# A depthwise convolution's shifted copies: through memory on GpSimd's queue, with two pointwise blocks ahead of the first convolution block

## The chip, the cores and the metric

The kernel runs on one core of a Trainium2 chip. The metric is the device time of one execution in microseconds (us); times of several runs are given as their median with the lowest and the highest. Engines are named as the profile names them: PE (TensorE), PEld (its weight loads), DVE (VectorE), ACT (ScalarE), POOL (GpSimd), SP (SyncE, which here only issues DMAs).

## The reference, cut to what matters

The reference is a decoder trunk of two layers on 256 positions of width 1024, in fp32. Each layer is a gated feed-forward network (FFN), a mixer, and another FFN, each with an adaLN modulation. The mixer of the second layer is a Conformer convolution module, and the change lies there:

```python
def conformer_conv(h, w_pw1, b_pw1, w_dw, b_dw, ln_g, ln_b, w_pw2, b_pw2):
    u = h @ w_pw1 + b_pw1                       # 1024 -> 2048
    a, g = jnp.split(u, 2, axis=-1)
    u = a * jax.nn.sigmoid(g)                   # GLU
    u = conv_general_dilated(u, w_dw[:, None, :], padding=[(30, 0)],
                             feature_group_count=1024) + b_dw   # depthwise, causal, width 31
    u = jax.nn.silu(layer_norm(u, ln_g, ln_b))
    return u @ w_pw2 + b_pw2
```

## The kernel before

The program's order on each engine is the order in which the Python code emits it (a manual schedule). All weights come from memory in one stream of half units of 512 KB. `issue` (line 191) asks for the next piece on SP's queue into one of six `raw` tiles (`RAW`), and `step` (line 208) consumes one: a weight is split into a rounded part `whi` (ACT, line 245) and a remainder `wlo` (DVE, line 220), an adaLN piece is folded into a sum by DVE (lines 284 and 286). Each `step` issues the piece six places on, whose slot it has just emptied. `high_part` emits the ACT copy up to one piece ahead of the step. The split units live in a ring of six (`RING`), and a unit can enter only when the unit six places before it has been used up (`uses`). `block` takes as many steps as a quota that `take` sets, and is called in each block of matmuls.

In `conv` the 1024 channels are eight blocks of 128. For a block b:

- `U(b)` (b from 4) or `UT` (b below 4) computes both halves of the first pointwise product `pw1` into PSUM. `U` takes one of two banks named `u`.
- `glu(b)` makes the sigmoid on ACT (`sg`, line 1065) and the gated product on DVE into one of four `ub` tiles (line 1066): 288 columns, 30 of them zeros ahead of the 256 positions.
- `spread(b)` makes the layout that the convolution wants: `R[b]`, in which the partitions are four shifts j of 32 channels, and the free axis is four groups g of channels. It is 16 DMAs from SBUF to SBUF, each 32 partitions by 284 columns, half on SP's queue and half on POOL's (line 1077).
- `wide(b)` expands the block's taps on POOL into `wd[b]` (line 1019; three buffers).
- `C(b)` is the convolution: 64 small matmuls over R[b] and wd[b] (line 1085), for a whole block or a half (128 positions), and an eviction with the bias on ACT into `v` (line 1089).
- `VT(b)` transposes `v` back (line 1099) for the layer norm's statistics.

SP's queue thus holds the weight stream and half of the spreads, in the order of the program. The blocks 0 to 3 pass `glu`, `spread` and `wide` ahead of the loop; the loop over b from 0 to 3 runs U(b + 4), glu(b + 4), C(b), spread(b + 4), wide(b + 3) and VT(b - 1); C(4) to C(7) follow, the last three in halves.

Of the kernel before, what the change touches and what calls it, by code (L numbers as in the profile page):

```python
# [8 lines left out]
F32 = mybir.dt.float32  # L9
# [5 lines left out]
P = 128  # L15
# [19 lines left out]
class Unit:  # L35
# [5 lines left out]
    def __init__(self, parts, uses=2):  # L41
        self.parts, self.uses = parts, uses
        self.hi = self.lo = None
        self.ready = 0
# [12 lines left out]
class Trunk:  # L57
    def __init__(self, ctx, tc, a):
        self.tc, self.nc, self.a = tc, tc.nc, a

        def pool(name, bufs=1, **kw):
            return ctx.enter_context(tc.tile_pool(name=name, bufs=bufs, **kw))

        self.const = pool("const")
        self.tiny = pool("tiny", 2)
        pool("pad").tile([P, 256], F32, name="pad")
        self.rawp = pool("rawp", RAW)
        self.hlp = pool("hlp", RING)
        self.keep = pool("keep")
        self.two = pool("two", 2)  # L70
        self.ps = pool("ps", 1, space=bass.MemoryType.PSUM)
        self.vecs = {(l, s, k): Vec(l, s, k) for l in range(2) for s in range(3) for k in range(3)}
        self.sums, self.open, self.pend, self.naccs = [], [], [], 0
        self.phase = 0
        self.ss, self.rs, self.zs = {}, {}, {}
        self.quota = self.credit = 0
        self.plan()
# [189 lines left out]
    def take(self, n=None):  # L267
        self.quota = PUMP[self.phase] if n is None else n
# [731 lines left out]
    def conv(self, cp, before, after):  # L1000
        nc, a = self.nc, self.a
        b1, bdw = self.col["b1"], self.col["bdw"]
        lng, lnb = self.col["lng"], self.col["lnb"]
        cols, take = self.cols, self.take
# [5 lines left out]
        ub = [cp.tile([P, 288], F32, name=f"ub{i}") for i in range(4)]  # L1010
# [4 lines left out]
        us, R, wd, yv, st, mv, rs = {}, {}, {}, {}, {}, {}, {}  # L1015

        def wide(b):
            wd[b] = cp.tile([P, 8, 4, 32], F32, name="wd", tag="wd", bufs=3)
            nc.gpsimd.tensor_tensor(
                wd[b], self.w2[:, :, 4 * b : 4 * b + 4].unsqueeze(3).to_broadcast([P, 8, 4, 32]),  # L1020
                mask.unsqueeze(1).unsqueeze(1).to_broadcast([P, 8, 4, 32]), op=ALU.mult,
            )

        def U(b):
            unit = self.pw1[b]
            self.need(unit)
            self.block()
            us[b] = self.bank("u")
            for s in range(2):
                out = us[b][:, s * T : s * T + T]  # L1030
                for k in range(KT):
                    cs = slice(k * 256 + s * P, k * 256 + s * P + P)
                    self.mm3(out, unit.hi[:, cs], unit.lo[:, cs], self.hh[:, k, :], self.hl[:, k, :], k == 0, k == KT - 1)
            unit.uses -= 1

        def UT(ps, b, t):

            unit = self.pw1[b]
            self.need(unit)
            self.block()  # L1040
            ts = slice(t * P, t * P + P)
            for k in range(KT):
                cs = slice(k * 256, k * 256 + 256)
                self.mm3(ps, self.hh[:, k, ts], self.hl[:, k, ts], unit.hi[:, cs], unit.lo[:, cs], k == 0, k == KT - 1)
            unit.uses -= 1

        def evac(ps):
            e = self.two.tile([P, 512], F32, name="z", tag="z", bufs=3)
            nc.scalar.activation(e, ps, AF.Copy)
            return e  # L1050

        def across(b, t, e, c):

            if b not in us:
                us[b] = self.bank("u")
            for s in range(2):
                nc.tensor.transpose(
                    us[b][:, s * T + t * P : s * T + t * P + P], e[:, c + s * P : c + s * P + P], self.ident
                )

        def glu(b):
            ps = us.pop(b)
            u = ub[b % 4]
            sg = cp.tile([P, T], F32, name="sg", tag="sg", bufs=2)
            nc.scalar.activation(sg, ps[:, T:], AF.Sigmoid, bias=cols[:, b1 + 8 + b : b1 + 9 + b])
            nc.vector.scalar_tensor_tensor(
                u[:, 30:286], ps[:, 0:T], cols[:, b1 + b : b1 + b + 1], sg, op0=ALU.add, op1=ALU.mult
            )

        def spread(b):  # L1070

            u = ub[b % 4]
            R[b] = cp.tile([P, 4, 284], F32, name="R", tag="R", bufs=4)
            for g in range(4):
                for j in range(4):
                    eng = nc.sync if (g + j) % 2 else nc.gpsimd
                    eng.dma_start(R[b][32 * j : 32 * j + 32, g, :], u[32 * g : 32 * g + 32, j : j + 284])  # L1077

        def C(b, t0=0, n=T):
            if ("v", b) not in us:  # L1080
                us["v", b] = cp.tile([P, T], F32, name="v", tag="v", bufs=3)
            ps = self.bank("m")[:, 0:n]
            for q in range(8):
                for g in range(4):
                    nc.tensor.matmul(  # L1085
                        ps[32 * g : 32 * g + 32, :], wd[b][:, q, g, :], R[b][:, g, 4 * q + t0 : 4 * q + t0 + n],
                        start=q == 0, stop=q == 7,
                    )
            nc.scalar.activation(
                us["v", b][:, t0 : t0 + n], ps, AF.Identity, bias=cols[:, bdw + b : bdw + b + 1]  # L1090
            )

        def VT(b, ts=(0, 1)):
            v = us["v", b]
            h, i = b // 4, b % 4
            for t in ts:
                if i == 0:
                    yv[t, h] = self.bank("y")
                nc.tensor.transpose(yv[t, h][:, i * P : i * P + P], v[:, t * P : t * P + P], self.ident)
            if i == 3:  # L1100
                for t in ts:
                    if h == 0:
                        st[t] = cp.tile([P, 2, 6], F32, name=f"st{t}")
                    nc.vector.bn_stats(st[t][:, h, :], yv[t, h])

        def moments(t):
            mv[t] = cp.tile([P, 2], F32, name=f"mv{t}")
            rs[t] = cp.tile([P, 1], F32, name=f"lr{t}")
            nc.vector.bn_aggr(mv[t], st[t])
            nc.vector.tensor_scalar(rs[t], mv[t][:, 1:2], EPS, None, op0=ALU.add)  # L1110
            nc.gpsimd.tensor_tensor(rs[t], rs[t], self.mhalf[:, 0:1], op=ALU.pow)

        def norm(t, h):
            z = self.two.tile([P, 512], F32, name="z", tag="z", bufs=3)
            nc.vector.tensor_scalar(z, yv[t, h], mv[t][:, 0:1], rs[t], op0=ALU.subtract, op1=ALU.mult)
            self.zs[t, h] = z
# [49 lines left out]
        UT(w[1][:, 256:], 2, 1)  # L1166
        across(0, 1, e, 0), across(1, 1, e, 256)
        e = evac(w[1])
        glu(0), spread(0), wide(0)
        UT(w[3][:, 256:], 3, 1)  # L1170
        f = evac(w[3])
        across(2, 0, e, 0), across(2, 1, e, 256)
        glu(1), spread(1), wide(1)
        across(3, 0, f, 0), across(3, 1, f, 256)
        glu(2), spread(2), wide(2)
        glu(3), spread(3)
        take(PUMP_LOOP)
        for b in range(4):
            U(b + 4)
            glu(b + 4)  # L1180
            C(b)
            spread(b + 4), wide(b + 3)
            if b:
                VT(b - 1)
                if b == 1:
                    nc.vector.tensor_tensor(b2, b2, gate, op=ALU.mult)
                else:
                    x = self.x[b - 2]
                    nc.vector.tensor_tensor(x, x, b2, op=ALU.add)
        nc.scalar.activation(warm, self.mhalf, AF.Silu)  # L1190
        self.block()
        C(4), wide(7), VT(3)
        self.need(self.pw2[3])
        take(5)
        C(5, 0, P), VT(4), self.block(), C(6, 0, P), VT(5, (0,)), C(7, 0, P), VT(6, (0,))
        C(5, P, P), VT(7, (0,)), moments(0), norm(0, 0), norm(0, 1)
        take(0)
        C(6, P, P), VT(5, (1,)), C(7, P, P), VT(6, (1,)), swish(0, 0), VT(7, (1,)), moments(1), put(0, 0)
# [64 lines left out]
```

## Time and profile before

| | |
|---|---|
| three runs, median (lowest to highest) | 1057.43 us (1055.07 to 1059.31) |
| the profiled execution, its own time | 1057.27 us |
| its span in the profile | 1055.5 us |
| PE, DVE, ACT, POOL busy, share of the span | 97%, 74%, 46%, 8% |
| moved by DMA | 254.92 MB, mean 242 GB/s |

The span is what the profile covers from the first instruction to the last; the execution's own time is 1.8 us longer. A busy share is a mean over the whole kernel. The convolution, at about 735 to 860 us, is one stage of it, and its own limits are read from that stretch of the trace.

### The profile page before, as it was taken

The page shows a single profiled execution, that of the slowest core. Times are in us where ns is not written, and L with a number is a line of the kernel's source. Part 1 is how long each engine was busy: PE and PEld are TensorE (multiplying, and loading weights), DVE is VectorE, ACT ScalarE, POOL GpSimd, SP SyncE. Part 2 cuts the span into 40 slices and gives each one's busy share as a digit, 9 for nine tenths or more (in the row PEclk, how much of TensorE's full clock was granted, in tenths as well). Part 3 has the DMA queues.
Part 4 walks back from the last instruction along what each step waited for, and adds up shares of the span by engine and source line. Part 5 has one row for each costly group of instructions (what it writes and reads, how often), then busy time and mean ns, then how long its engine had stood idle before and what let it go on. Part 6 is the DMA issues. An engine that isn't in the chain of part 4 may idle for free.

```text
span 1055.5 us, 14925 instructions
## 1 busy us (share of the span) xinstructions
PE 1020.3 (97%) x5510; PEld 826.7 (78%) x5510; DVE 785.3 (74%) x1165; ACT 489.6 (46%) x763; POOL 86.8 (8%) x149
## 2 busy tenths in 40 slices
PE   8999999999999999999999999999995899999998
PEld 5778787877776788878878878888984688888886
DVE  5679888978997798878578878776747669556643
ACT  3454444555685544444454444454621356434420
POOL 3000000002210000000020000000484200000000
PEclk9999999999999999999999999999998999999999
DMA  8989999948676399999739889894667427776711
GB/s 299 316 273 333 305 341 321 324 140 284 220 241 194 106 329 313 308 309 315 233 105 315 290 297 312 276 307 136 193 201 227 159 80 259 259 234 193 231 40 40
DMA packets 186812, 254.92 MB, mean 242 GB/s; under 512 B 10437, under 2 KB 136166, under 8 KB 186740
## 3 DMA queue, kind: packets, MB, share of 16 engines
q1 hardware_dynamic: 183856, 250.88, 72.1%
q0 software_dynamic: 2736, 3.04, 1.0%
q8 instruction: 43, 0.70, 0.3%
q14 instruction: 29, 0.24, 0.1%
q10 hardware_dynamic: 148, 0.06, 0.0%
HBM read 248.24 MB, written 1.05 MB: 236 GB/s over the span
## 4 chain that ended last, share of the span: by engine, by line
PE 79%; DVE 7%; DMA 5%; ACT 3%; issue 3%; POOL 2%; SPq 1%; DVEq 0%; ACTq 0%; POOLq 0%
PE u L666 14%; PE u L664 14%; PE u L665 14%; PE y L664 10%; PE y L666 10%; PE y L665 10%; DMA raw<-in_ffn_w_in_dram 2%; DMA raw<-in_ada_w_dram 2%; DVE wlo L220 2%; PE m L742 2%; ACT whi L245 1%; POOL R L1077 1%; PE m L1085 1%; ACT p L893 1%; DVE x L601 1%
## 5 line engine op out<-in xcount | busy, mean ns | idle before, releaser
L220 DVE TENSOR_TENSOR wlo<-raw,whi 128x1024 fp32r<-128x1024 f32 x320 | 389.2, 1244 | 51.1 <-ACT whi L245 50.8
L245 ACT ACTIVATE whi<-raw 128x1024 fp32r<-128x1024 f32 x320 | 329.1, 1055 | 178.1 <-DMA raw<-in_ffn_w_in_dram 96.2
L664 PE MATMUL u<-whi,hh 128*128 128x512 f32 x672 | 266.7, 397 | 1.2 <-ACT hh L587 1.2
L666 PE MATMUL u<-whi,hl 128*128 128x512 f32 x672 | 263.1, 391 | 0.0
L665 PE MATMUL u<-wlo,hh 128*128 128x512 f32 x672 | 261.8, 390 | 0.0
L286 DVE SCALAR_TENSOR_TENSOR acc<-raw,sc,acc 128x512 f32<-128x512 f32 x224 | 168.0, 750 | 6.7 <-DMA raw<-in_ada_w_dram 1.7
L666 PEld LDWEIGHTS u<-whi,hl 128*128 128x128 f32 x672 | 126.1, 188 | 29.6 <-DVE hl L588 1.7
L664 PEld LDWEIGHTS u<-whi,hh 128*128 128x128 f32 x672 | 126.2, 188 | 28.7 <-ACT hh L587 2.9
L665 PEld LDWEIGHTS u<-wlo,hh 128*128 128x128 f32 x672 | 126.4, 188 | 25.0
L664 PE MATMUL y<-whi,gh 128*128 128x512 f32 x352 | 138.5, 393 | 0.2 <-ACT gh L750 0.2
L666 PE MATMUL y<-whi,gl 128*128 128x512 f32 x352 | 137.3, 390 | 0.0
L665 PE MATMUL y<-wlo,gh 128*128 128x512 f32 x352 | 137.1, 389 | 0.0
L664 PE MATMUL y<-whi,hh 128*128 128x512 f32 (+1 forms) x256 | 96.9, 379 | 0.2 <-ACT hh L934 0.2
L666 PE MATMUL y<-whi,hl 128*128 128x512 f32 (+1 forms) x256 | 93.9, 367 | 0.0
L665 PE MATMUL y<-wlo,hh 128*128 128x512 f32 (+1 forms) x256 | 93.5, 365 | 0.0
L751 DVE TENSOR_TENSOR gl<-m,gh 128x512 fp32r<-128x512 f32 (+1 forms) x48 | 31.0, 647 | 83.7 <-ACT gh L750 83.5
L750 ACT ACTIVATE gh<-m 128x512 fp32r<-128x512 f32 (+1 forms) x48 | 27.0, 563 | 131.9 <-PE m L742 131.8
L712 ACT ACTIVATE sg<-u 128x256 f32<-128x256 f32 x84 | 32.1, 383 | 106.6 <-PE u L666 106.6
L664 PEld LDWEIGHTS y<-whi,gh 128*128 128x128 f32 x352 | 66.1, 188 | 15.7 <-ACT sg L712 1.7
L666 PEld LDWEIGHTS y<-whi,gl 128*128 128x128 f32 x352 | 66.1, 188 | 14.4 <-DVE gl L751 0.4
L665 PEld LDWEIGHTS y<-wlo,gh 128*128 128x128 f32 x352 | 66.1, 188 | 13.4
L620 POOL TENSOR_TENSOR r<-v,mhalf 128x1 f32<-128x1 f32 x12 | 6.6, 554 | 671.9 <-DVE v L619 671.9
(169 smaller groups left out, 944.6 us busy)
## 6 DMA issues: line engine op xcount, KB each, us to landing
raw<-in_ffn_w_in_dram SPq DMA_DIRECT2D x164, 512.0 KB, 5.1
raw<-in_ada_w_dram SPq DMA_DIRECT2D x144, 512.0 KB, 5.1
raw<-in_ffn_w_out_dram SPq DMA_DIRECT2D x88, 512.0 KB, 5.3
raw<-in_attn_w_qkv_dram SPq DMA_DIRECT2D x24, 512.0 KB, 4.9
raw<-in_conv_w_pw_dram SPq DMA_DIRECT2D x24, 512.0 KB, 5.1
raw<-in_ffn_w_in_dram SPq DMA_DIRECT2D x24, 256.0 KB, 5.7
raw<-in_attn_w_o_dram SPq DMA_DIRECT2D x8, 512.0 KB, 4.3
gate<-in_ada_b_dram SPq DMA_DIRECT2D x6, 512.0 KB, 6.7
```

The costliest lines, as they stand in the source:

```text
L220: (eng or nc.vector).tensor_tensor(lo, raw, hi.bitcast(F32), op=ALU.subtract)
L245: self.nc.scalar.activation(hi, self.like(self.raws[i], hi), AF.Copy)
L286: nc.vector.scalar_tensor_tensor(dst, raw[:, i, :], self.sc[:, k : k + 1], dst, op0=ALU.mult, op1=ALU.add)
L601: nc.vector.tensor_tensor(x[:, s], x[:, s], tmp, op=ALU.add)
L664: nc.tensor.matmul(out, lh, rh, start=start, stop=False)
L665: nc.tensor.matmul(out, lh, rl, start=False, stop=False)
L666: nc.tensor.matmul(out, ll, rh, start=False, stop=stop)
L712: nc.scalar.activation(sg, ps[:, 0:256], AF.Silu)
L742: nc.tensor.transpose(ps[:, o : o + P], g[:, t, k * P : k * P + P], self.ident)
L750: nc.scalar.activation(hi, src, AF.Copy)
L751: nc.vector.tensor_tensor(lo, src, hi.bitcast(F32), op=ALU.subtract)
L893: nc.scalar.activation(p[:, c0:c1], p[:, c0:c1], AF.Exp, bias=st[:, t : t + 1], scale=-1.0, accum_out=st[:, 2 + t : 3 + t],)
```

## The change

`spread(b)` is split in two. A new `park(b)`, emitted right after `glu(b)`, writes the block's `ub` tile (128 x 288) to a tile in device memory with one DMA on POOL's queue. `spread(b)` then reads it back with four DMAs on the same queue, one for each shift j: 32 partitions by four groups by 284 columns. SP's queue has no part in it any more. In the order of work, U(4) is emitted ahead of the loop and the loop runs U(b + 5), so that U(4) and U(5) both stand ahead of C(0); `park(b + 4)` stands ahead of C(b) and `spread(b + 4)` behind it. One `block()` moves from ahead of C(4) to behind VT(3), and with it `take(5)` and one `block()` further on are dropped.

```diff
+        self.dram = pool("dram", space=bass.MemoryType.DRAM)
...
+        drams = {}
+
+        def park(b):
+
+            drams[b] = self.dram.tile([P, 288], F32, name=f"d{b}")
+            nc.gpsimd.dma_start(drams[b], ub[b % 4])
+
         def spread(b):
 
-            u = ub[b % 4]
+            d = drams[b]
             R[b] = cp.tile([P, 4, 284], F32, name="R", tag="R", bufs=4)
-            for g in range(4):
-                for j in range(4):
-                    eng = nc.sync if (g + j) % 2 else nc.gpsimd
-                    eng.dma_start(R[b][32 * j : 32 * j + 32, g, :], u[32 * g : 32 * g + 32, j : j + 284])
+            for j in range(4):
+                src = bass.AP(tensor=d.tensor, offset=d.offset + j, ap=[[288, 32], [288 * 32, 4], [1, 284]])
+                nc.gpsimd.dma_start(R[b][32 * j : 32 * j + 32, :, :], src)
...
-        glu(0), spread(0), wide(0)
+        glu(0), park(0), spread(0), wide(0)
...
-        glu(1), spread(1), wide(1)
+        glu(1), park(1), spread(1), wide(1)
...
-        glu(2), spread(2), wide(2)
-        glu(3), spread(3)
+        glu(2), park(2), spread(2), wide(2)
+        glu(3), park(3), spread(3)
         take(PUMP_LOOP)
+        U(4)
         for b in range(4):
-            U(b + 4)
-            glu(b + 4)
+            if b < 3:
+                U(b + 5)
+            glu(b + 4), park(b + 4)
             C(b)
             spread(b + 4), wide(b + 3)
...
-        self.block()
         C(4), wide(7), VT(3)
         self.need(self.pw2[3])
-        take(5)
-        C(5, 0, P), VT(4), self.block(), C(6, 0, P), VT(5, (0,)), C(7, 0, P), VT(6, (0,))
+        self.block()
+        C(5, 0, P), VT(4), C(6, 0, P), VT(5, (0,)), C(7, 0, P), VT(6, (0,))
```

## Rows read from the trace of the kernel before

**Rows 1.** The page, busy time by engine: us, share, instructions.

```profile
PE 1020.3 (97%) x5510; PEld 826.7 (78%) x5510; DVE 785.3 (74%) x1165; ACT 489.6 (46%) x763; POOL 86.8 (8%) x149
```

**Rows 2.** Busy time by stretch; granted clock, DMA share and GB/s stand last.

```profile
802.00:814.00 12.00, 0.42 (x9) 0.06 (x1) 8.36 (x12) 1.88 (x4) 5.01 (x8) 0.72 0.79 270
814.00:818.00 4.00, 4.00 (x66) 3.43 (x66) 2.36 (x4) 2.45 (x3) 3.41 (x7) 0.57 0.99 295
818.00:822.00 4.00, 0.56 (x3) 0.29 (x2) 3.81 (x3) 2.73 (x4) 3.98 (x4) 0.86 1.05 348
```

**Rows 3.** PE in order of time: start, duration, work [idle before, releaser].

```profile
794.74 3.66 PE L1085 MATMUL m<-R,wd 128*32 128x256 f32 x64
...
798.70 3.66 PE L1085 MATMUL m<-R,wd 128*32 128x256 f32 x64
813.94 0.69 PE L1099 MATMUL y<-ident,v 128*128 128x128 f32 x2 [11.58 <-ACT v L1089]
814.56 3.52 PE L1085 MATMUL m<-R,wd 128*32 128x128 f32 x64
821.52 0.69 PE L1099 MATMUL y<-ident,v 128*128 128x128 f32 x2 [3.44 <-ACT v L1089]
...
827.26 1.91 PE L1085 MATMUL m<-R,wd 128*32 128x128 f32 x58 [0.25 <-DMA R<-ub]
```

**Rows 4.** ACT in order of time, around the long wait.

```profile
812.10 1.06 ACT L245 ACTIVATE whi<-raw 128x1024 fp32r<-128x1024 f32 x1 [21.86 <-DMA raw<-in_ffn_w_in_dram]
...
813.42 0.47 ACT L1089 ACTIVATE v<-m,cols 128x256 f32<-128x256 f32 x1
```

**Rows 5.** SP's queue in order of time, from the loop's start.

```profile
761.38 0.98 SPq L205 DMA_DIRECT2D raw<-in_conv_w_pw_dram  x2
762.46 18.23 SPq L1077 DMA_DIRECT2D R<-ub  x24
...
803.50 0.51 SPq L205 DMA_DIRECT2D raw<-in_ffn_w_in_dram  x1
```

**Rows 6.** POOL in order of time: two DMAs at the start, the first spread.

```profile
4.27 0.75 POOL L402 DMA_DIRECT2D ab<-in_ada_b_dram  x1
...
10.23 0.48 POOL L421 DMA_DIRECT2D rows<-in_attn_g_k_dram  x1 [1.71 <-DMA ab<-in_ada_b_dram]
...
756.72 3.94 POOL L1077 DMA_DIRECT2D R<-ub  x8 [15.48 <-DVE ub L1066]
```

**Rows 7.** DMA issues: count, KB each, median us from issue to landing.

```profile
out_dram<-x SPq DMA_DIRECT2D x4, 128.0 KB, 1.7
...
ab<-in_ada_b_dram POOLq DMA_DIRECT2D x1, 36.0 KB, 5.7
```

**Rows 8.** POOL's DMAs of 128 short pieces (line 987): ns, min/median/max.

```profile
L987 POOL DMA_DIRECT2D tq<-in_conv_w_dw_dram x8: 548/551/618, 546.9 to 551.3; - x8
```

**Rows 9.** Line 1019 (`wide`) alone by stretch: length, POOL busy, clock, DMA, GB/s.

```profile
755.00:830.00 75.00, 17.79 (x8) 0.91 0.71 221
```

**Rows 10.** POOL's spreads in three stretches: ns of one, us to landing.

```profile
L1077 POOL DMA_DIRECT2D R<-ub x8: 496/497/527, 756.7 to 760.2; - x8
DMA to landing us min/median/max: 1.8/2.3/2.8
...
L1077 POOL DMA_DIRECT2D R<-ub x8: 496/498/529, 762.5 to 766.0; - x8
DMA to landing us min/median/max: 5.3/6.0/6.6
...
L1077 POOL DMA_DIRECT2D R<-ub x11: 496/496/529, 775.5 to 780.4; - x11
DMA to landing us min/median/max: 1.7/1.9/2.4
```

**Rows 11.** The page's groups for DVE's two steps: busy us, mean ns.

```profile
L220 DVE TENSOR_TENSOR wlo<-raw,whi 128x1024 fp32r<-128x1024 f32 x320 | 389.2, 1244 | 51.1 <-ACT whi L245 50.8
...
L286 DVE SCALAR_TENSOR_TENSOR acc<-raw,sc,acc 128x512 f32<-128x512 f32 x224 | 168.0, 750 | 6.7 <-DMA raw<-in_ada_w_dram 1.7
```

## Prediction

> **What bounds the kernel now.** I read the page first. TensorE (PE) is busy for 97% of the span [rows 1], so a gain has to come out of a hole in PE, or out of work on PE, and the change touches no matmul. Next I asked for the busy time by stretch around the convolution. There is one large hole: between 802 and 814 us PE works 0.42 us of 12, and the granted clock falls from 1.00 to 0.72 in that stretch and 0.57 in the next, so it lies between its two levels of 2.4 and 1.2 GHz after PE has stood still [rows 2]. The time-ordered list of PE says what the hole is [rows 3]. C(3) starts at 794.74, C(4) ends at 802.36, and then the transposes VT(3) wait 11.58 us for ACT's `v`; VT(4) waits 3.44 us more. C(5)'s first half takes 3.52 us at the low clock, where C(7)'s takes 1.91 us for 58 of its 64 matmuls, so 2.1 us for all: the clock costs 1.4 us there.
>
> Why is ACT late? It executes in program order, and in front of `sg` of block 7 and of C(3)'s eviction stands a `whi` copy that waits 21.86 us for a weight load [rows 4]. That load was asked for at 803.50, late, because SP's queue holds the weight loads and half of the spreads: 24 spread DMAs occupy it from 762.46 for 18.23 us, and no weight load leaves in that time [rows 5]. A late load is consumed late, its slot (the raw tiles have six) comes free late, and the next load is late too. So the loop's bound is a chain over SP, the DMA engines, VectorE and ACT, not PE.
>
> What could be had at most: without waits, PE would be at C(3) at the same 794.74 (in either order U(4) to U(7) and C(0) to C(2) lie before it), C(3) and C(4) with a transpose are 3.96 us each by the distance of their starts, a half of C(5) or C(6) with its transposes about 2.15. C(7)'s first half would start near 794.7 + 7.9 + 4.3 = 806.9. Before it (its main part) starts at 827.26 [rows 3]. The hole is worth 20 us, 1.9% of the time.
>
> **The change part by part.** SP loses 64 spread DMAs. Nothing of the spread is left on it, so weight loads leave as soon as a slot is free. POOL loses 64 spread DMAs and gains 8 parks and 32 reads. U(5) goes ahead of C(0), which reorders PE's work and removes none. The `block()` behind C(4) instead of ahead of it takes three `whi` copies from in front of C(4)'s eviction, which is the second wait (3.44 us). `take(5)` sets what the quota is already: nothing. The parks add 8 x 147 KB of writes and keep the volume of the reads (4.65 MB): at most 1.2 MB of 255.
>
> The new cost is a wait that was nowhere before. A read of the copy in memory can be issued only when the park has landed, and POOL executes in order, so POOL stands still for the landing of each park; queued behind it are the reads, the next `wide` (C's weights), and the next park. Who waits for those is PE: C(b) needs R[b] and wd[b]. Before, POOL issues eight DMAs without a stop in 3.94 us [rows 6]; the same rows show a POOL DMA that does wait for a landing, and it starts about 0.25 us after it (issued 4.27, 5.7 to landing [rows 7], next start 10.23).
>
> So I sum POOL's chain from park(0) at 756.72, the start of the first spread [rows 6], to the end of wide(7), on which the last C depends:
> - reads: 32, each 128 rows of 1.1 KB. The nearest row is POOL's DMA of 128 short pieces, 0.55 us [rows 8]; 32 x 0.55 = 17.6 us. (Below: 0.497 as the 32-row spreads, 15.9; above: 0.75, the slowest that POOL issues anywhere [rows 6], 24.)
> - wides: eight, 17.8 us in all, taken as they are [rows 9].
> - wake-ups: 8 x 0.25 = 2.0 us.
> - landings of the parks, L each. No row shows a store from POOL. From below: POOL's spreads with no weight load under way land in 1.7 to 2.4 us [rows 10], stores to memory by SP in 1.7 [rows 7]; I take 2.0. From above: POOL's spreads with two or more loads under way take 5.3 to 6.6 [rows 10]; I take 6.0.
>
> End of wide(7) = 756.72 + 17.6 + 17.8 + 2.0 + sum of L = 794.1 + sum of L. With all eight at 2.0 this is 810.1; each park that lands behind weights adds 4.0. That is the whole question: how many parks, N, meet a busy DMA.
>
> SP's freedom makes them meet it. VectorE consumes a half unit in 1.24 us and an adaLN piece in 2 x 0.75 us [rows 11]. The 14 loads that SP issued from 761.38 to 803.50 [rows 5], and some four behind them, are now asked for from 757 to about 793, one per 1.5 to 2 us at 0.5 MB, with 0.73 MB of park and reads every 9 us: near 350 GB/s, which is what a stretch with the DMA engines fully busy moves (348 at a share of 1.05 [rows 2]). Two or more are then mostly in flight. My estimates, park by park, from those rows: park 0 at 756.7 with one load under way, 2.8 (that group's longest [rows 10]); park 1 at 764, the stream starting, 4.5; parks 2 and 3, 6.0 each; park 4 near 792, as the stream runs out, 4.5; 5 and 6, 2.0; 7 meets the loads that the moved `block()` lets go, 2.8. Sum 30.6, which is N = 3.65.
>
> End of wide(7) = 824.7, against a start of C(7) at 827.26 before. One low clock is paid again, since C(6) comes after a wait about as long as the 3.44 us one; before two halves ran low, and I charge 1.4 us. Gain 827.26 - 1.4 - 824.7 = 1.2 us. In general it is 15.8 - 4.0 N.
>
> What hides the rest: C(1) to C(3) have wd from near 772, 783 and 800 us, so PE's first wait moves to C(3), where there was none; it costs nothing of its own, since the end is set by wide(7). glu(4) stands behind U(5)'s block now, but that block can take only two steps (the next unit's slot is U(5)'s own), some 2.5 us on VectorE that lie beside U(5). Were POOL's chain short, these 2.5 us would lie on PE's path. After the convolution nothing changes: the ring of split units holds the same ones either way, since its next unit needs a slot that O(0, 0) frees.
>
> The Trainium skill, in "DMA: Bandwidth & Descriptors", section on the anatomy of one DMA on the GpSimd path, gives about 2.0 us plus bytes over 436 GB/s for one DMA. For a park of 147 KB this makes an estimate of 2.34 us, a sum of L of 18.7, and a gain of 13.1 us. This trace agrees only where no load is under way (1.7 to 2.4) and shows 5.3 to 6.6 where they are. The same page's rules for kernel authors speak against the change: a DMA that reads what an earlier one wrote has to wait for the first one's semaphore before it is issued. No run here shows what happens without that wait.
>
> **The rivals.**
> - Fast: parks land as on an idle DMA (N up to 2.6), since loads spaced evenly may leave gaps. For it: in the three stretches shown, 19 of 27 of POOL's spreads land in 1.7 to 2.8 us [rows 10]. Against: in just those stretches SP was jammed, which is what is removed. N = 1.5 gives 9.8 us, 1047.5; N = 0 would give 1041. It decides below N = 2.6. The estimate of 2.34 us above belongs here. Chance 0.29.
> - Slow: POOL becomes the bound outright. Freed, SP keeps two or more loads in flight in the whole loop, and every park and the reads ahead of it in POOL's own queue take 6 us or more (N = 6: 8.2 us, 1065.5; N = 8: 1073.5). It decides above N = 5.3; reads at 0.75 us instead of 0.55 add 6.4 us, like 1.6 parks. For it: up to 6.6 us with only two loads ahead [rows 5, 10]. Against: the ring has only six slots and SP is silent after about 795. Chance 0.25.
> - It doesn't do what it says: the loads were late because VectorE frees slots late, not because SP is jammed. Then the 21.86 us wait of ACT stays, the loads are spread out, the parks land early, and the time is that of before, 1057. Against: 18.23 us of SP in one piece. Chance 0.04.
> - My forecast, POOL's chain replaces ACT's wait at about the same length (N from 2.6 to 5.3). Chance 0.42.
>
> **How the numbers follow.** The sum stands against the profiled execution, 1057.27 us with a span of 1055.5, which lies 0.16 below the median of the three runs. 1057.27 - 1.2 = 1056.1, so 1056. Half a per cent, 5.3 us, is about what a measurement of this kernel can tell from no change. The forecast's own N makes 1052 to 1063; the range takes in the fast case down to N = 1.2 (1046) and the slow one up to N = 5.9 (1065). Faster 0.29; same 0.42 + 0.04 = 0.46; slower 0.25.
>
> **What would show it right or wrong.** Right: SP has no spread and its loads run without a pause over 0.5 us of its own making until about 795; ACT's wait of 21.86 us is gone; POOL's reads wait for the park's landing, near 30 us in the loop; PE waits for `wd` or R from C(3) on; wide(7) ends near 825. The reads take 0.55 us each on POOL. Wrong: the sum of POOL's waits is below 25 or above 41 us; PE waits first for `ub` (glu(4)) or for a weight; reads take longer than 0.55; or the first half of C(7) starts before 817.

## The result and the profile after

The changed kernel takes 1068.26 us (median of six, 1064.63 to 1069.87) against 1058.37 us of the kernel before in the same sessions (median of six): a ratio of 1.0095, 95% interval 1.0069 to 1.0121. It is slower by 9.9 us, and outside the range of the prediction. The profiled executions are 12.6 us apart by their spans (1068.1 against 1055.5), so they show the loss somewhat large.

The page says first that PE does the same work and has more holes (answer to [rows 1]):

```profile
PE 1022.0 (96%) x5510; PEld 827.7 (77%) x5510; DVE 778.2 (73%) x1165; ACT 489.8 (46%) x763; POOL 74.8 (7%) x125
```

PE in order of time, the matmuls of the convolution (answer to [rows 3]; all lines of the program stand one to seven lower than before, so `C` is L1092 and `wide` L1020):

```profile
792.00 3.66 PE L1092 MATMUL m<-R,wd 128*32 128x256 f32 x64 [0.87 <-issue]
...
807.07 5.24 PE L1092 MATMUL m<-R,wd 128*32 128x256 f32 x64 [11.04 <-POOL wd L1020]
...
815.78 3.66 PE L1092 MATMUL m<-R,wd 128*32 128x256 f32 x64 [3.10 <-POOL wd L1020]
...
822.44 1.96 PE L1092 MATMUL m<-R,wd 128*32 128x128 f32 x64 [2.63 <-POOL wd L1020]
...
830.38 3.64 PE L1092 MATMUL m<-R,wd 128*32 128x128 f32 x64 [5.62 <-POOL wd L1020]
...
837.14 3.24 PE L1092 MATMUL m<-R,wd 128*32 128x128 f32 x64 [2.76 <-DMA R<-d]
```

From the top these are C(2), C(3), C(4) and the first halves of C(5), C(6) and C(7). PE is free for C(3) at 796.03 (807.07 less the wait), 1.3 us after C(3) started before. Then it waits for POOL at each of C(3) to C(6), 22.4 us in all, and once more for the reads of R[7]. The two waits for ACT's `v` (11.58 and 3.44 us) are gone. C(7) starts at 837.14, and the main part of it started at 827.26 before: 9.9 us later.

POOL in order of time, the whole chain (answer to [rows 6]; L1076 is a park, L1084 the four reads, L1020 a `wide`):

```profile
756.96 0.57 POOL L1076 DMA_DIRECT2D d<-ub  x1 [15.44 <-DVE ub L1067]
761.21 2.21 POOL L1084 DMA_DIRECT2D R<-d  x4 [3.69 <-DMA d<-ub]
763.44 2.02 POOL L1020 TENSOR_TENSOR wd<-w,mask 128x1024 f32<-128x1024 f32 x1
765.42 0.60 POOL L1076 DMA_DIRECT2D d<-ub  x1
771.11 2.18 POOL L1084 DMA_DIRECT2D R<-d  x4 [5.09 <-DMA d<-ub]
...
775.16 0.60 POOL L1076 DMA_DIRECT2D d<-ub  x1
782.06 2.18 POOL L1084 DMA_DIRECT2D R<-d  x4 [6.30 <-DMA d<-ub]
...
786.11 0.60 POOL L1076 DMA_DIRECT2D d<-ub  x1
793.27 2.18 POOL L1084 DMA_DIRECT2D R<-d  x4 [6.56 <-DMA d<-ub]
795.44 0.56 POOL L1076 DMA_DIRECT2D d<-ub  x1
802.90 2.18 POOL L1084 DMA_DIRECT2D R<-d  x4 [6.89 <-issue]
805.10 1.92 POOL L1020 TENSOR_TENSOR wd<-w,mask 128x1024 f32<-128x1024 f32 x1
...
826.21 2.18 POOL L1084 DMA_DIRECT2D R<-d  x4 [3.29 <-issue]
828.41 3.78 POOL L1020 TENSOR_TENSOR wd<-w,mask 128x1024 f32<-128x1024 f32 x2
```

Read the line of 805.10: this is `wide(3)`, which needs nothing of the park and read in front of it. It comes when POOL comes to it, and it ends at 807.02; C(3) starts at 807.07. Not all of C(3)'s wait is due to it: R[3], read from 793.27 on, landed only at about 802 (its last read took 7.1 us, below), so C(3) lacked both until then and the taps alone for the last 5 us. The last line is wide(6) and wide(7), which end at 832.19.

SP's queue in order of time (answer to [rows 5]) holds nothing but weight loads; ACT's copy of the FFN weight waits 7.57 us, not 21.86 (answer to [rows 4]):

```profile
741.73 25.18 SPq L206 DMA_DIRECT2D raw<-in_conv_w_pw_dram  x11
767.71 14.81 SPq L206 DMA_DIRECT2D raw<-in_ada_w_dram  x8
783.73 41.28 SPq L206 DMA_DIRECT2D raw<-in_ffn_w_in_dram  x8
```

```profile
793.14 1.06 ACT L246 ACTIVATE whi<-raw 128x1024 fp32r<-128x1024 f32 x1 [7.57 <-DMA raw<-in_ffn_w_in_dram]
```

So the jam was there and the change removed it. The price is in the DMA engines. Busy time by stretch, 765 to 795 us, first of the kernel before and then of the changed one (last three columns: granted clock, DMA share, GB/s):

```profile
765.00:795.00 30.00, 30.00 (x355) 24.54 (x357) 16.67 (x12) 7.37 (x11) 25.90 (x40) 1.00 0.63 187
```

```profile
765.00:795.00 30.00, 29.13 (x340) 24.67 (x342) 24.09 (x28) 7.11 (x10) 12.02 (x18) 1.00 1.02 308
```

The engines went from 0.63 busy to full for 30 us, at 308 GB/s, and they stay full until 802 (a share of 1.08 from 795 to 800). The list of DMA issues by stretch shows what a transfer meets there (median us to landing): park 2, park 4, the last read of R[3], and the reads of R[7].

```profile
d<-ub POOLq DMA_DIRECT2D x1, 144.0 KB, 6.6
...
d<-ub POOLq DMA_DIRECT2D x1, 144.0 KB, 6.9
R<-d POOLq DMA_DIRECT2D x1, 142.0 KB, 7.1
...
R<-d POOLq DMA_DIRECT2D x4, 142.0 KB, 8.8
```

### The profile page after: what moved, and what is told of

Same layout as the page of the kernel before. It is cut to its first block, busy times and chain, and to the rows that moved or that the text cites. A ratio compares the mean times of both kernels' runs of the same rounds, so it can differ in the third digit from the quotient of the medians.

```text
span 1068.1 us, 14719 instructions
## 1 busy us (share of the span) xinstructions
PE 1022.0 (96%) x5510; PEld 827.7 (77%) x5510; DVE 778.2 (73%) x1165; ACT 489.8 (46%) x763; POOL 74.8 (7%) x125
## 5 line engine op out<-in xcount | busy, mean ns | idle before, releaser
L221 DVE TENSOR_TENSOR wlo<-raw,whi 128x1024 fp32r<-128x1024 f32 x320 | 383.8, 1228 | 39.8 <-ACT whi L246 39.7
L1092 PE MATMUL m<-R,wd 128*32 128x128 f32 (+1 forms) x704 | 34.7, 358 | 26.0 <-POOL wd L1020 22.4
```

The costliest lines, as they stand in the source:

```text
L221: (eng or nc.vector).tensor_tensor(lo, raw, hi.bitcast(F32), op=ALU.subtract)
L1092: nc.tensor.matmul(ps[32 * g : 32 * g + 32, :], wd[b][:, q, g, :], R[b][:, g, 4 * q + t0 : 4 * q + t0 + n], start=q == 0, stop=q == 7,)
```

## The experiments

The theory: in POOL's program order each `wide`, and so each C, stands behind the landing of a park, and parks land late because the freed weight stream fills the DMA engines. The rivals: the new order of work costs it; the traffic itself costs it (reads late, not taps); POOL's own reads make the park late. Twelve kernels ran, each beside the kernel before.

**mem_only.** The kernel before with `park` and the new `spread`, in the old order of work.

```diff
             U(b + 4)
-            glu(b + 4)
+            glu(b + 4), park(b + 4)
             C(b)
             spread(b + 4), wide(b + 3)             # the new spread, from memory
```

> The memory part alone: park and four reads on GpSimd's queue, in the order of work of the kernel before. Theory (POOL's chain: each wide, and so each C, stands in program order behind the landing of a park): the chain is the same as in the changed kernel, so the time is too, 1064 to 1071 us, with POOL's waits for parks near 40 us in sum. Rival (the new order of work costs it): near the kernel before, 1056 to 1061.

Measured: 1066.99 us, ratio 1.0083 (1.0056 to 1.0111). As the theory has it, the memory part alone loses what the whole change loses. PE's waits, in total, number and longest:

```profile
PE m L1092 <- POOL wd L1020: 20.2, 4, 8.0
PE m L1092 <- DMA R<-d: 3.2, 1, 3.2
```

**order_only.** The changed kernel's order with the old spreads.

```diff
-        glu(0), park(0), spread(0), wide(0)        # new spread
+        glu(0), spread(0), wide(0)                 # old spread; no park anywhere
```

> The new order alone: U(4) and U(5) ahead of C(0), the moved block, but the spreads from SBUF to SBUF on both queues as before. Theory: nothing waits for a park, SP's queue is as jammed as before, and the second wait of the kernel before (3.44 us) goes; 1052 to 1059 us. Rival (the order costs it): 1064 to 1070.

Measured: 1058.02 us, ratio 1.0012 (0.9994 to 1.0029). The order costs nothing, and wins nothing either. ACT in order of time shows that the hole only moves: `sg` of block 4 (783.98) now stands behind a copy that waits 14.25 us, and PE waits 11.7 us for `ub` ahead of U(6).

```profile
783.01 1.06 ACT L245 ACTIVATE whi<-raw 128x1024 fp32r<-128x1024 f32 x1 [14.25 <-DMA raw<-in_conv_w_pw_dram]
783.98 0.46 ACT L1065 ACTIVATE sg<-u,cols 128x256 f32<-128x256 f32 x1
```

**wide_first.** The changed kernel with `wide` in front of the reads.

```diff
-        glu(0), park(0), spread(0), wide(0)
+        glu(0), park(0), wide(0), spread(0)
...
-            spread(b + 4), wide(b + 3)
+            wide(b + 3), spread(b + 4)
```

> The changed kernel with wide emitted between park and its reads, so that the 1.9 us of each wide lie beside the landing. Theory: POOL's chain loses 8 x 1.9 = 15 us and C(3) no longer waits for its taps; C(7) starts 12 to 15 us earlier than 837, so 1053 to 1057 us. Rival (the reads from memory and the traffic are late, not the taps): 1065 to 1069.

Measured: 1061.51 us, ratio 1.0032 (1.0014 to 1.0049). Seven of the expected 12 to 15 us came, and the time lies between the two ranges. No wait for taps is left among PE's waits, as the theory has it, but waits for R came in their place, as the rival has it: the end moved from the taps to the reads, which land 3 to 9 us after they are issued.

```profile
PE m L1092 <- DMA R<-d: 17.9, 4, 8.4
```

**no_wait.** The reads take the input x instead of the parked copy, so the convolution works on data that are not the GLU's.

```diff
-                src = bass.AP(tensor=d.tensor, offset=d.offset + j, ap=...)
+                src = bass.AP(tensor=xin.tensor, offset=xin.offset + (b % 4) * P * 288 + j, ap=...)
```

> The changed kernel, but the four reads take their data from the input x instead of the parked copy, so that POOL has nothing to wait for; the parks are still written, nobody reads them, and the convolution works on data that are not the GLU's. Same DMAs, same bytes. Theory: POOL's 40 us of waits go, PE runs the loop almost without a wait, C(7) starts near 810: 1040 to 1046 us. Rival (the traffic itself is the cost: more bytes, reads of memory beside the weight loads): 1060 or more, with waits of PE for R.

Measured: 1046.68 us, ratio 0.9897 (0.9870 to 0.9923). With the same DMAs and the same bytes, but without POOL's wait, the loss of 9.9 us is a gain of 10.7. That settles the main question: the wait for the park's landing costs about 21 us (2.0% by the two ratios). The transfers themselves did not get faster: reads land in 7.8 us and parks in 6.9 (medians from about 757 on), against 4.6 and 4.8 in the changed kernel. What costs is that POOL stands still for the landing. The time is 0.7 us above the theory's range, and PE still waits 7.3 us for `ub` ahead of U(7):

```profile
PE u L665 <- DVE ub L1067: 7.3, 1, 7.3
```

**quiet_loop.** The changed kernel with the weight stream held still in the loop.

```diff
-PUMP_LOOP = 5
+PUMP_LOOP = 0
...
-        self.block()                               # behind VT(3)
+                                                   # twelve steps behind C(7) instead
```

> The changed kernel with PUMP_LOOP = 0 and no block in the loop: the weight stream stands still while POOL works (it is caught up by twelve steps behind the convolution, so the total time is worse and is not what is read). Read: the landing of parks 1 to 7. Theory (weight loads in flight make a park land late): 2.0 to 3.0 us each with none in flight, POOL's waits in sum near 20 us instead of 38, wide(7) ends 10 to 18 us earlier than 832. Rival (POOL's own reads ahead of the park in its queue make it late): parks still land in 4 to 7 us.

Measured: parks 1 to 3 land in 2.1 us, against 5.4, 6.6 and 6.9; wide(7) ends at 815.56, 16.6 us earlier. The total, 1068.05 in one run, has the late weights in it and says nothing here. Without loads in flight, POOL's own reads do not make these three parks late. Of the others, 5 and 6 land in 2.1 us, 0 in 4.4 beside the last loads of the stretch ahead, and 7 in 3.8 with a load beside it. Park 4 takes 4.5 us: it follows the four reads of R[3] with no `wide` between, and lands 0.2 us after the last of them, 3 us after the one load beside it. In the changed kernel, too, park 4 lands 0.4 us after the last read of R[3]. So the reads ahead in the queue have a part in it where loads or a short distance keep them in flight, and no run separates the two. POOL in order of time, parks 1, 2 and 4:

```profile
764.16 0.60 POOL L1076 DMA_DIRECT2D d<-ub  x1
766.52 2.18 POOL L1084 DMA_DIRECT2D R<-d  x4 [1.76 <-DMA d<-ub]
...
770.58 0.60 POOL L1076 DMA_DIRECT2D d<-ub  x1
772.94 2.18 POOL L1084 DMA_DIRECT2D R<-d  x4 [1.76 <-DMA d<-ub]
...
781.55 0.56 POOL L1076 DMA_DIRECT2D d<-ub  x1
786.54 2.18 POOL L1084 DMA_DIRECT2D R<-d  x4 [4.43 <-issue]
```

**late_block.** The changed kernel with its one `block()` behind C(7)'s first half.

```diff
-        self.block()
-        C(5, 0, P), VT(4), C(6, 0, P), VT(5, (0,)), C(7, 0, P), VT(6, (0,))
+        C(5, 0, P), VT(4), C(6, 0, P), VT(5, (0,)), C(7, 0, P), VT(6, (0,)), self.block()
```

> The changed kernel with its one block behind VT(3) moved behind C(7)'s first half, so that the four weight loads which it lets go are asked for later. Theory: the reads of R[7], 8.8 us under those loads, land in about 3 us; PE's wait for R[7] (2.76 us) and the half clock around it go; park 7 lands 1 to 2 us earlier; 3 to 7 us in all, 1061 to 1065 us. Rival (the last reads are not on the path): 1067 to 1069.

Measured: 1065.82 us, ratio 1.0070 (1.0045 to 1.0095), 2.4 us below the changed kernel's median, where 3 to 7 were expected. The two intervals overlap, so the times alone do not show a gain. The trace does: PE no longer waits for R[7], and C(7) starts at 833.52 instead of 837.14. The waits for `wd` remain:

```profile
PE m L1092 <- POOL wd L1020: 19.4, 4, 9.9
```

**early_parks.** The same DMAs, with parks 0 to 3 ahead of all reads and each `wide` ahead of its reads.

```diff
-        glu(0), park(0), spread(0), wide(0)
+        glu(0), park(0), wide(0)
...
-        glu(2), park(2), spread(2), wide(2)
-        glu(3), park(3), spread(3)
+        glu(2), park(2)
+        glu(3), park(3)
+        spread(0), wide(1), spread(1), wide(2), spread(2), spread(3)
...
-            spread(b + 4), wide(b + 3)
+            wide(b + 3), spread(b + 4)
```

> The same DMAs as in the changed kernel in another order on POOL: parks 0 to 3 as soon as their ub is there, then the reads, and wide ahead of the reads everywhere. Theory: almost every landing lies beside other work of POOL; wide(7) and the reads of R[7] end before 815, C(7) starts near 812: 1040 to 1050 us. Rival (traffic): 1060 or more.

Measured: 1058.42 us, ratio 1.0013 (0.9997 to 1.0030). All of the loss is back, but none of the hole: a miss by 8 us or more. POOL in order of time shows why in two places. Reads 11 to 16 now wait for earlier reads to land, so that park 4 comes at 779.89; and POOL still waits for the landing of parks 4 to 7 behind the `wide`. The first of these waits is the program's own: its POOL DMAs take eight semaphores in turn, and each of these reads starts 0.3 us after the landing of the POOL DMA eight places ahead (read 11, at 772.23, after read 3, which was issued at 762.88 and took 9.1 us). POOL thus has at most eight DMAs under way.

```profile
772.23 0.55 POOL L1084 DMA_DIRECT2D R<-d  x1 [1.21 <-DMA R<-d]
...
779.89 0.58 POOL L1076 DMA_DIRECT2D d<-ub  x1 [0.91 <-DMA R<-d]
780.49 1.93 POOL L1020 TENSOR_TENSOR wd<-w,mask 128x1024 f32<-128x1024 f32 x1
787.57 2.20 POOL L1084 DMA_DIRECT2D R<-d  x4 [5.15 <-DMA d<-ub]
```

**early_late.** early_parks and late_block together (both diffs above).

> early_parks with the block behind C(7)'s first half as well. Theory: 0 to 4 us faster than early_parks, since the last reads meet no loads. Rival: no difference.

Measured: 1055.59 us, ratio 0.9983 (0.9967 to 1.0000), 2.8 us below early_parks: as expected, though the two intervals just touch.

**early_pump4.** early_late with one step fewer per block in the loop.

```diff
-PUMP_LOOP = 5
+PUMP_LOOP = 4
...
+        take(5), self.block()                      # behind C(7)'s first half
```

> early_late with PUMP_LOOP = 4 in place of 5, so that the loop's blocks end one step short of the FFN's first weight and its whi copy (10.8 us of waiting on ACT in early_parks, in front of glu(6) and C(2)'s eviction) is emitted behind C(7)'s first half. Theory (what is left of the hole in early_parks is that wait: it makes ub6, park 6 and R[6] late): PE's waits for R[6] and R[7] shrink, 1047 to 1053 us. Rival (the DMA engines are simply full of reads and weights): within 2 us of early_late, 1055.6.

Measured: 1055.73 us, ratio 0.9969 (0.9956 to 0.9982). ACT's wait for the FFN weight is gone and the time did not follow: the rival's 2 us. Of the kernels that do all the work it has the lowest ratio, 0.3% under the kernel before, but its interval does not part it from early_late or from copies_pump4 below. The DMA engines are full there too, from 765 to 795 us, at 274 GB/s:

```profile
765.00:795.00 30.00, 26.04 (x282) 22.65 (x281) 20.68 (x17) 7.36 (x11) 19.39 (x25) 1.00 1.04 274
```

**no_wait_pump4.** no_wait with the same edit of the steps and the block behind C(7)'s first half (reads from x).

> no_wait (reads from the input x, not from the parked copy) with PUMP_LOOP = 4 and the block behind C(7)'s first half: both waits taken away, POOL's for parks and ACT's for the late FFN weight (13.6 us in no_wait, of which PE felt 7.3 us). Theory: PE runs from U(4) to C(7) almost without a wait: 1037 to 1042 us, which is the whole hole. Rival: still near 1046.

Measured: 1047.58 us, ratio 0.9890 (0.9870 to 0.9910): the rival. ACT's wait for the FFN weight is gone, VectorE still waits for the adaLN pieces (4.5 us in all, 6.3 in no_wait), and PE still waits 4.5 us for `ub`. The loads themselves are late: the eight adaLN pieces land in 13.7 us (median), against 5.2 in the kernel before and 5.7 in the changed one, where POOL's waits hold the reads back.

```profile
raw<-in_ada_w_dram SPq DMA_DIRECT2D x8, 512.0 KB, 13.7
```

**copies_pump4.** order_only with the same edit of the steps and the block behind C(7)'s first half; no memory copy.

> order_only (spreads from SBUF to SBUF on both queues) with PUMP_LOOP = 4 and the block behind C(7)'s first half: no memory copy, and only the order of the weight steps changed. Theory (SP's jam itself makes the loads late, so that ACT waits 14 us for a pw2 weight ahead of glu(4) however few steps are taken): 1054 to 1059 us. Rival (the hole of before is only the FFN weight's copy in front of the evictions): 1045 to 1050 us.

Measured: 1057.00 us, ratio 0.9977 (0.9962 to 0.9992). As the theory has it: with the spreads on SP's queue the loads are late however few are taken, and ACT still waits 13.9 us for a pointwise weight.

**no_wait_half.** no_wait without the reads of blocks 4 to 7 (their convolution uses what blocks 0 to 3 read).

```diff
+            if b >= 4:
+                R[b] = R[b - 4]
+                return
```

> no_wait with the reads of blocks 4 to 7 left out as well (these blocks convolve what blocks 0 to 3 read), so 2.3 MB less traffic in and behind the loop. Open: what holds no_wait at 1046.7, 5 to 8 us above PE without waits. Theory (the DMA engines are full from 765 to 795, at about 300 GB/s, so the weight loads themselves are late and with them glu(5)): the loads land earlier, PE's wait of 7.3 us for ub shrinks to under 3, 1040 to 1044 us. Rival (VectorE and ACT set the pace of the weight steps): 1046 to 1048 with the same wait.

Measured: 1041.27 us, ratio 0.9848 (0.9824 to 0.9873). Half of the reads less is 5.4 us less. PE's longest wait for `ub` is 3.5 us where under 3 was expected, in place of 7.3, and the adaLN pieces land in 10.9 us (median) in place of 14.2 in no_wait. The engines are still full from 765 to 795 (a share of 1.01, 302 GB/s), but less of what they move is reads. So the reads' traffic accounts for a little over half of the 10 us by which no_wait misses a time without the hole (1057 less 20).

## Why the prediction was wrong

The mechanism was the forecast's: SP's jam goes, ACT's long wait with it, and POOL's serial chain of park, landing, reads and `wide` sets the end, seen by PE as a wait for taps from C(3) on. Each of these is in the profile, and no_wait takes the chain's wait out and finds 21.6 us (1068.3 to 1046.7; 20.9 by the ratios). What failed were one term of the sum and one step of the path.

**The landings, park by park.** The prediction put them at 2.8, 4.5, 6.0, 6.0, 4.5, 2.0, 2.0 and 2.8 us, 30.6 in all. The list of DMA issues gives 4.0, 5.4, 6.6, 6.9, 6.9, 4.1, 2.1 and 3.3: 39.3, which in the prediction's count is N = 5.8, not 3.65, and beyond the 5.3 at which the slow rival decides. From the start of a park to the start of its reads, which adds the wake-ups (0.25 us each in the prediction, 0.4 here), it is 42.6 us instead of 32.6. Of these 37.9 are idle in the trace and the rest is the issue of the parks; the sign set for being wrong, waits above 41 us, is met by the first count and not by the second. The reads are as forecast (0.545 us each, 17.5 in sum against 17.6), the wides 15.4 instead of 17.8. So wide(7) ends at 832.2, not 824.7.

The two ends taken for a landing, 2.0 and 6.0, were about right: 2.1 with no load in flight (quiet_loop), up to 6.9 with them. What was wrong is how full the busy stretch is and how long it lasts. The prediction called its demand near 350 GB/s and just what the engines move. Its own terms, 0.5 MB per 1.5 to 2 us and 0.73 MB per 9 us, come to 331 to 414, and the rows that give 348 at a share of 1.05 for 4 us give 295 at 0.99 for the 4 us before [rows 2]. With this mix the engines moved 308 at a share of 1.02, 302 in no_wait and 274 in early_pump4. So the demand did not fit, the stretch ran on to 802, and park 4 met it in full.

Park 5, 2.1 us of the miss, is another case: it was issued at 806.95, when the loads had stopped, and it still took 4.1 us. Between 808 and 811 the DMA queues moved nothing but the park and one 16 KB packet of an instruction queue:

```profile
q0 software_dynamic: 48, 0.15, 13.2%
q8 instruction: 1, 0.02, 3.0%
```

By the packets' times, 30 of the park's 32 data packets had moved by 808.7; the last two came at 809.83 and 810.31, when the 16 KB packet (808.40 to 809.84) was done. That they waited for it fits, but is not shown.

The Trainium skill, in "DMA: Bandwidth & Descriptors", section on the anatomy of one DMA on the GpSimd path, would have made each park an estimate of 2.34 us. quiet_loop's 2.1 and park 6's 2.1 agree with it, and the changed kernel's 4.0 to 6.9 for parks 0 to 5 do not. The same page's section on issuing engines says that DMAs from all queues run on the same 16 engines and interleave, and that was the rule to size by; this trace agrees with it, since parks on POOL's queue land late beside loads on SP's.

**"The end of wide(7), on which the last C depends."** That was one condition of two. The reads of R[7], which the prediction took for landed in time, were issued from 826.21 on, just as the moved `block()` had let loads go, and took 8.8 us; C(7) started 5.0 us after wide(7) ended. late_block takes those loads away, and PE's wait for R[7], 2.8 us, goes. By the prediction's formula the landings alone (N = 5.8) make 1065, still inside its range; this second condition and the clock carried the time out of it.

Together: from the 824.7 of the forecast to the start of C(7) at 837.14 it is 12.4 us: landings and wake-ups 10.0, wides -2.4, the late R[7] 5.0 (reads -0.1). The low clock was charged once, at 1.4 us, and came at three of PE's waits: C(3), C(6) and C(7) run at 5.24, 3.64 and 3.24 us after waits of 11.04, 5.62 and 2.76, where C(4) takes 3.66 and C(5)'s half 1.96. But PE waits again right behind C(3) and C(6), so that only C(7)'s 1.3 us lie on the path, about as charged. It came a fourth time behind the convolution, after a stretch in which PE was busy 4.31 of 5 us; the kernel before has a clock of 1.00 there (836 to 866), and most of what is left of the 12.6 us between the two spans, beyond the 9.9 and the 1.3, falls there. Why the clock fell there is not shown.

```profile
850.00:855.00 5.00, 4.91 (x19) 3.97 (x20) 3.46 (x9) 1.50 (x4) 0.00 (x0) 0.66 0.00 0
```

The fast rival is answered too: N up to 2.6 needs quiet DMA engines. quiet_loop has them (23.0 us of landings, N = 1.8), but only by not loading weights. And no run passes the bound of the hole's 20 us: no_wait_half, without the wait and with half of the reads, is 16.7 us faster than the kernel before.

Left open: whether reads of longer rows would fill the engines less, and so give the unjammed SP its gain with a real copy. That was not tried.

## What to carry to other kernels

A round trip through memory on an in-order queue is priced by the landing that the queue waits for, not by the bytes: put everything that does not need the landing (here `wide`) ahead of the wait, and read the landing from a stretch as busy as the one that the change will make, not as the one that it finds. When a jam on one queue is removed, work out the DMA engines' share with the jammed loads moved together; parks 1 to 3 landed in 2.1 us at a share of 0.46 (quiet_loop, 765 to 795) and in 5.4 to 6.9 at 1.02. And taking one engine's wait away pays little while the same full resource feeds the next: without ACT's wait for the FFN weight, VectorE still waited for its adaLN pieces, and PE behind it (early_pump4 and no_wait_pump4, neither faster for it).

## What the runs showed of the hardware

With the DMA engines full, what they moved varied with the mix: 308 GB/s at a share of 1.02 (changed kernel, 765 to 795; 253 to 408 in stretches of 5 us at shares of 0.96 to 1.08), 274 at 1.04 (early_pump4), 348 at 1.05 in a stretch of the kernel before [rows 2]. A store of 147 KB from POOL's queue landed in 2.1 us with no load in flight (quiet_loop, parks 1 to 3), in 5.4 to 6.9 on full engines (changed kernel, parks 1 to 4), and once in 4.1 with no load moving (park 5).
